# Opening three feed-forward layers with two of the seven products of many blocks

## The chip, the cores and the metric

The kernel runs on one core of a Trainium2 chip. The metric is the device time of one execution in microseconds (us). Engine names are those of the profile: PE is TensorE (matrix products), DVE is VectorE, ACT is ScalarE, POOL is GpSimd, SP is SyncE, which here only issues DMAs.

## What is computed

Two layers of a network on 256 context and 512 latent tokens of width 1024. Each layer is feed-forward, mixer, feed-forward, each behind a modulation by shift, scale and gate vectors made from a conditioning vector, and each closed by a layer norm. The part that matters here:

```python
def swiglu(h, w_in, w_out):
    a, b = jnp.split(h @ w_in, 2, axis=-1)
    return (jax.nn.silu(a) * b) @ w_out

def ffn_substep(x, mods, w_in, w_out, g, b):
    shift, scale, gate = mods
    y = swiglu(modulate(x, shift, scale), w_in, w_out)
    return layer_norm(ALPHA * x + MACARON * gate * y, g, b)
...
m_lat = jnp.split((c_act @ w_ada[layer] + b_ada[layer])[:, None, :], N_MOD, axis=-1)
```

The hidden width is 2816, so `w_in` has 2 x 22 blocks of 128 columns. There are four feed-forward layers, called here (0,0), (0,1), (1,0) and (1,1). The first three work on all 768 tokens, the last on the 512 latent ones.

## The kernel before

All products are made in three passes: each fp32 operand is split into a rounded part (ACT cast, L117) and the remainder (DVE subtraction, L119), and `mm3` issues h*h, h*l and l*h (L157 to L159). `xh` and `xl` hold the split input, 8 tiles of 128 rows by 768 tokens.

The first half of a feed-forward layer makes gate and up rows of 22 hidden blocks. A **plain** block is 2 x 8 x 3 products on all tokens, made in the two token halves of the layer norm before (512 and 256 tokens; 256 and 256 in (1,1)). The other blocks are made by one level of Strassen's scheme in Winograd's form (`seven`): seven products of 4 x 3 matmuls on half the tokens (384; 256 in (1,1)) instead of eight. Its weight sums are made per block on POOL (`ahead`, L673 to L675, and L684), two blocks ahead, then split by ACT and DVE (`operands`); its input sums once per layer (`sums_of_inputs`: POOL adds at L650, DVE subtractions at L648, splits). Results leave PSUM by ACT copies and DVE additions (L712, L711), and `put` multiplies gate and up (L583, L587), which keeps one token half in `spare` tiles and stores the other (`late_g`).

Before the change, (0,1) and (1,0) open with 4 plain blocks and (1,1) with 5. The reason is the layer norm of the step before: its second token half is still being normalized (`pending`, drained by `settle`) while PE works on the first half, and the input sums need both.

Beside the products, `ada` makes the modulation vectors: per block of 128 columns a 512 KB load and one DVE product with a sum (L185) for each of one or two conditioning vectors. A list of sections for each layer says which vectors are made beside its first half (tiles `spare`) and which beside its second half (tiles `six`). Beside the first half two blocks of such columns are made per hidden block, until the list is done.

Every engine executes its own instructions in a fixed order, which is set when the program is built; the orders shown below are of built programs.

Of the kernel before, what the change touches and what calls it, by code (L numbers as in the profile page):

```python
# [12 lines left out]
F32 = mybir.dt.float32  # L13
F32R = mybir.dt.float32r
BF16 = mybir.dt.bfloat16
AF = mybir.ActivationFunctionType
# [3 lines left out]
P = 128  # L20
D = 1024
KB = D // P
NCTX = 256
NLAT = 512
NT = NCTX + NLAT
# [17 lines left out]
class Net:  # L43
    def __init__(self, tc, ctx, ins, out):
# [35 lines left out]
        self.RB = None  # L80
# [143 lines left out]
    def start(self, pool):  # L224
# [33 lines left out]

        w = lambda q: [load(self.ins["w_ada0"][q, i]) for i in range(KB // 2)]
# [6 lines left out]
        for j in range(KB):  # L266
# [8 lines left out]
            self.split(self.xh[:, j, :], self.xl[:, j, :], x_)  # L275
            if j % 2 and q < 4:
                columns(q, quarter)
# [21 lines left out]
    def layer_norm(self, half, halves, aff, nxt, ax_new, r_of, s1, done, table):  # L299
        nc = self.nc  # L300
# [26 lines left out]
        for j in range(KB):  # L327
            r = r_of(half, j)
            nc.vector.tensor_mul(out=r, in0=r, in1=rs[:, :n])  # L329
            if nxt is not None:  # L330
# [8 lines left out]
                self.split(self.xh[:, j, c0:c1], self.xl[:, j, c0:c1], h[:, :n])  # L339
            g, b = aff[:, 0, j:j + 1], aff[:, 1, j:j + 1]  # L340
# [27 lines left out]
    def out_phase(self, pool, nk, wsrc, gload, halves, gate, l, i, nxt, r_of, table=None, keep=False, ada=iter(())):  # L368
# [3 lines left out]
        aff = self.affine(l, i, nxt)  # L372
        ax_new = None
        if nxt is not None:
            self.n += 1
            ax_new = self.dram.tile([P, KB, NT], F32, name=f"ax{self.n}")
        nh = nk // 2
# [33 lines left out]
        for n_step, (half, kk) in enumerate(steps):  # L411
# [33 lines left out]
            if half:  # L445
                for _ in norm:
                    pass
            s1 = self.sums(n)
# [34 lines left out]
    def residual(self, r, j, c0, c1):  # L483
# [5 lines left out]
        nc.scalar.mul(out=r, in_=r, mul=ALPHA)  # L489

# [66 lines left out]
    def ffn(self, l, p, halves, nxt, ada=((), ()), table=None, first_of_all=False):  # L557
# [5 lines left out]
        plain = 4 if n > 512 else 5  # L563
        in_ada, out_ada = (list(a) for a in ada)
        with ExitStack() as st:
# [72 lines left out]
            def sums_of_inputs():  # L638

                t1 = [self.spare(pool)[:, :2 * m].rearrange("p (k c) -> p k c", k=2) for _ in range(2)]  # L640
# [3 lines left out]
                for k in range(4):  # L644
                    hi = lambda K, N: B(K, N)[0][:, k, :].bitcast(F32)
                    lo = lambda K, N: B(K, N)[1][:, k, :].bitcast(F32)
# [6 lines left out]
                    a = t1[k // 2][:, k % 2, :]  # L653
                    sub(a, b12, hi(0, 0))
                    sub(a, a, lo(0, 0))
# [22 lines left out]
            def operands(raw, sums):  # L678
# [4 lines left out]
                w = self.pair(raw[0], 1024)  # L683
                nc.gpsimd.tensor_sub(out=a12, in0=a12, in1=sums[:, 512:])  # L684
                yield part(w, 0), part(w, 1)
# [8 lines left out]

            def seven(x, now, coming, before):
# [4 lines left out]

                def grow(ps, w, b):

                    first = ps is None
                    ps = self.ps()[:, :m] if first else ps
                    for k in range(4):
                        ks = slice(k * P, (k + 1) * P)
# [677 lines left out]
```

## Time and profile before

| what | before |
|---|---|
| median of 3 runs (lowest to highest) | 2761.87 us (2758.68 to 2762.24) |
| the profiled execution | 2759.16 us |
| its span, first to last instruction | 2757.4 us |
| mean granted TensorE clock in it | 0.992 |
| PE busy | 2662.5 us, 97% |
| DVE busy | 1964.8 us, 71% |
| ACT, POOL busy | 1219.8 us, 891.0 us |

Busy shares are means over stages with different limits. Here the stage that matters is the first half of a feed-forward layer, and in it the time of one block on each engine.

### The profile page before, as it was taken

To read this page: it belongs to the slowest core of one execution; us is meant where nothing else is said; L and a number is where in the kernel's file an instruction comes from. 1 tells how busy PE (TensorE), PEld (TensorE's weight loads), DVE (VectorE), ACT (ScalarE), POOL (GpSimd) and SP (SyncE) were. 2 spreads that over 40 slices of the span, in tenths; PEclk is the share of its full clock that TensorE was granted. 3 is DMA by queue.
4 is the path that set the end of the run, shared out by engine and by line. 5 is a ranking of instruction groups with operands and counts; after the bars stand their busy time and mean duration, and the time that the engine had idled before them with its cause. 6 is when DMAs were issued, how large, how long until landed. Compare 5 with 4: busy or idle time off the path is not lost. (4 is left out here: it accounts for less than half of the span.)

```text
span 2757.4 us, 43916 instructions
## 1 busy us (share of the span) xinstructions
PE 2662.5 (97%) x17372; PEld 2429.0 (88%) x17372; DVE 1964.8 (71%) x2917; ACT 1219.8 (44%) x1919; POOL 891.0 (32%) x686
## 2 busy tenths in 40 slices
PE   8999999999989999999999999999999998999997
PEld 6999988987778789999889999988887777999997
DVE  4899677847764779977786676556727776787665
ACT  3433433634442544343254444423534655555554
POOL 2545300522210564440044444201422211466302
PEclk9999999999999999999999999999999999999998
DMA  6343266521104334426653432265521012423563
GB/s 250 138 154 123 94 233 233 202 87 68 46 22 166 109 132 147 140 88 221 218 199 121 166 127 79 92 231 194 204 77 47 35 39 85 134 102 119 173 218 116
DMA packets 138770, 374.20 MB, mean 136 GB/s; under 512 B 16066, under 2 KB 47170, under 8 KB 138564
## 3 DMA queue, kind: packets, MB, share of 16 engines
q1 hardware_dynamic: 136832, 370.21, 38.3%
q8 instruction: 136, 2.23, 0.3%
q10 hardware_dynamic: 1732, 1.20, 0.2%
q14 instruction: 70, 0.57, 0.1%
HBM read 337.78 MB, written 33.56 MB: 135 GB/s over the span
## 5 line engine op out<-in xcount | busy, mean ns | idle before, releaser
L117 ACT CAST r4h<-raw 128x1024 fp32r<-128x1024 f32 (+1 forms) x322 | 332.7, 1035 | 627.5 <-PE ps L158 320.3
L157 PE MATMUL ps<-xh,r4h 128*128 128x512 f32 (+2 forms) x1732 | 584.3, 339 | 11.1 <-ACT xh L117 7.7
L158 PE MATMUL ps<-xl,r4h 128*128 128x512 f32 (+2 forms) x1732 | 580.8, 336 | 0.5 <-DVE xl L119 0.4
L159 PE MATMUL ps<-xh,r4l 128*128 128x512 f32 (+2 forms) x1732 | 580.5, 336 | 0.4 <-DVE r4l L119 0.4
L119 DVE TENSOR_TENSOR r4l<-raw,r4h 128x1024 fp32r<-128x1024 f32 (+1 forms) x306 | 374.2, 1225 | 223.0 <-ACT r4h L117 161.7
L157 PEld LDWEIGHTS ps<-xh,r4h 128*128 128x128 f32 x1732 | 327.1, 189 | 40.6 <-ACT xh L117 10.2
L158 PEld LDWEIGHTS ps<-xl,r4h 128*128 128x128 f32 x1732 | 327.9, 189 | 23.0 <-DVE xl L119 2.0
L159 PEld LDWEIGHTS ps<-xh,r4l 128*128 128x128 f32 x1732 | 327.6, 189 | 22.1 <-DVE r4l L119 0.8
L157 PE MATMUL ps<-six,r4h 128*128 128x384 f32 (+1 forms) x852 | 278.5, 327 | 6.6 <-ACT c L712 6.5
L157 PE MATMUL ps<-r4h 128*128 128x512 f32 (+1 forms) x768 | 275.7, 359 | 1.1 <-DVE g L827 1.1
L158 PE MATMUL ps<-six,r4h 128*128 128x384 f32 (+1 forms) x852 | 276.1, 324 | 0.0
L159 PE MATMUL ps<-r4h,r4l 128*128 128x512 f32 (+1 forms) x768 | 275.5, 359 | 0.2
L159 PE MATMUL ps<-six,r4l 128*128 128x384 f32 (+1 forms) x852 | 275.5, 323 | 0.0
L158 PE MATMUL ps<-r4l,r4h 128*128 128x512 f32 (+1 forms) x768 | 275.2, 359 | 0.0
L159 PE MATMUL ps<-r4h,spare 128*128 128x256 f32 (+1 forms) x896 | 262.2, 293 | 10.1 <-DVE spare L119 10.0
L157 PE MATMUL ps<-r4h,spare 128*128 128x256 f32 (+1 forms) x896 | 265.5, 296 | 4.0 <-ACT spare L117 4.0
L158 PE MATMUL ps<-r4l,spare 128*128 128x256 f32 (+1 forms) x896 | 261.3, 292 | 0.0
L684 POOL TENSOR_TENSOR raw<-raw,late 128x512 f32<-128x512 f32 x71 | 93.6, 1318 | 400.7 <-DVE r4l L119 397.2
L119 DVE TENSOR_TENSOR r4l<-late,r4h 128x1024 fp32r<-128x1024 f32 x71 | 106.1, 1494 | 115.1 <-PE ps L158 95.5
L159 PEld LDWEIGHTS ps<-r4h,spare 128*128 128x128 f32 x896 | 174.4, 195 | 13.6 <-DVE spare L119 11.7
L157 PEld LDWEIGHTS ps<-r4h,spare 128*128 128x128 f32 x896 | 174.5, 195 | 8.6 <-ACT spare L117 4.6
L185 DVE SCALAR_TENSOR_TENSOR trash<-spare 128x1024 bf16<-128x1024 f32 x112 | 179.3, 1603 | 1.3 <-DMA spare<-in_w_ada 1.3
(289 smaller groups left out, 5637.9 us busy)
## 6 DMA issues: line engine op xcount, KB each, us to landing
raw<-in_w_ffn_in SPq DMA_DIRECT2D x176, 512.0 KB, 3.6
raw<-in_w_ffn_out SPq DMA_DIRECT2D x176, 512.0 KB, 4.1
spare<-in_w_ada SPq DMA_DIRECT2D x80, 512.0 KB, 5.6
six<-in_w_ada SPq DMA_DIRECT2D x64, 512.0 KB, 5.5
g<-late_g SPq DMA_DIRECT2D x88, 128.0 KB, 2.1
six<-g SPq DMA_DIRECT2D x44, 256.0 KB, 3.8
raw<-in_w_in_even SPq DMA_DIRECT2D x20, 512.0 KB, 3.5
raw<-in_w_in_odd SPq DMA_DIRECT2D x16, 512.0 KB, 3.4
```

What stands on the lines that cost most here:

```text
L117: self.copied = self.nc.scalar.copy(out=h, in_=src)
L119: eng.tensor_sub(out=l, in0=src, in1=h.bitcast(F32))
L157: mm(out=ps, lhsT=h, rhs=xh, start=first, stop=False)
L158: mm(out=ps, lhsT=h, rhs=xl, start=False, stop=False)
L159: mm(out=ps, lhsT=l, rhs=xh, start=False, stop=last)
L185: nc.vector.scalar_tensor_tensor(out=self.tmp("trash").bitcast(BF16), in0=r, scalar=1.0, in1=self.c_bc[v], op0=ALU.mult, op1=ALU.mult, acc ...
L684: nc.gpsimd.tensor_sub(out=a12, in0=a12, in1=sums[:, 512:])
```

## The change

In (0,1), (1,0) and (1,1) there are no plain blocks any more. The layer opens with the first two of the seven products, A11*B11 and A12*B21, of 10 blocks (14 in (1,1)); both need only the first half of the tokens. The first product is copied and stored to DRAM (`p1s`), the sum of both goes through the activation into the gate's place (`G`). Then `five` makes the other five products of these blocks, with the first one loaded back, and `seven` the rest. The layer norm (and the start of the kernel) also stores the unsplit input to DRAM (`whole`), from which `sums_of_inputs` loads four quarters in place of POOL's additions and one of the DVE subtractions. The sections of modulation vectors are dealt out anew, and the layer norm's `affine` is made at the end of the first token half, since its inputs can now be made beside the same layer's second half.

```diff
-        plain = 4 if n > 512 else 5
+        plain, opened = (4, 0) if first_of_all else (0, 10 if n > 512 else 14)
...
-                    for t, q in ((b12, (0, 1)), (b22, (1, 1)), (b21, (1, 0))):
-                        nc.gpsimd.tensor_add(out=t, in0=hi(*q), in1=lo(*q))
+                    for t, (K, N) in ((a, (0, 0)), (b12, (0, 1)), (b22, (1, 1)), (b21, (1, 0))):
+                        nc.sync.dma_start(out=t, in_=self.whole[:, K * 4 + k, cols[N]])
...
-                    sub(a, b12, hi(0, 0))
-                    sub(a, a, lo(0, 0))
+                    sub(a, b12, a)
...
-                w = self.pair(raw[0], 1024)
+                if not opened:
+                    w = self.pair(raw[0], 1024)
                 nc.gpsimd.tensor_sub(out=a12, in0=a12, in1=sums[:, 512:])
...
+            def opening(sums):
+                wt = [self.weights(ws[2 * x]) for x in range(3)]
...
+                def first_product(x):
+                    X[x] = grow(None, part(x, 0), B(0, 0))
+                    t = self.tmp("p1")[:, :m]
+                    copy(t, X[x])
+                    nc.sync.dma_start(out=p1s[:, x, :], in_=t)
+
+                first_product(0)
+                for x in range(opened):
+                    if x + 1 < opened:
+                        first_product(x + 1)
+                    grow(X[x], part(x, 1), B(1, 0))
+                    if x < 2:
+                        self.settle(None if x else 9)
+                    else:
...
+                                    nc.scalar.activation(out=G(i)[:, 0, :m], in_=X.pop(i), func=AF.Silu)
+                        self.settled = None
+                        next(sums, None)
+                    if x + 3 < opened:
+                        wt.append(self.weights(ws[2 * x + 6]))
...
+            def five(x, now, coming, before):
+
+                (S2, S1), S4 = now[0][:2]
+                if x % 2 == 0:
+                    load_p1(x + 2)
+                p1 = p1_of.pop(x)
+                u2, p5 = (self.tmp("c")[:, :m] for _ in range(2))
+                X = grow(None, S2, made[2])
+                add(u2, p1, X)
+                before()
...
+                Y = grow(None, S1, made[1])
+                add(p5, p1, Y)
+                more(coming)
+                grow(X, S3, made[3])
+                add(p5, p5, X)
+                next(ada, None)
+                more(coming)
+                grow(Y, S4, B(1, 1))
+                add(u2, u2, Y)
+                nc.scalar.activation(out=u2, in_=u2, func=AF.Silu)
+                put(x, m, n, u2, p5)
+
+                def rest():
+                    grow(X, A22, made[4])
+                    add(p1, p1, X)
+                    put(x, 0, m, G(x)[:, 0, :m], p1)
...
-        net.ffn(0, 1, FULL, (1, 0, (LAT, CTX)), (each(0, 8, 9) + each(1, 0, 2), each(1, 2, 5)), SILU)
-        net.ffn(1, 0, FULL, (1, 3, (LAT, CTX)), (each(1, 5, 7), each(1, 7, 9)))
+        net.ffn(0, 1, FULL, (1, 0, (LAT, CTX)), (each(0, 8, 9) + each(1, 0, 1), each(1, 1, 3)), SILU)
+        net.ffn(1, 0, FULL, (1, 3, (LAT, CTX)), (each(1, 3, 5), each(1, 5, 8)))
...
-        net.ffn(1, 1, LATS, None)
+        net.ffn(1, 1, LATS, None, (each(1, 8, 9), ()))
```

How this moves instructions shows in the order on three places. The first is DVE in layer (0,1), in a hidden block that makes modulation vectors beside it. Before, twelve of the fourteen rows of one `seven` block (a split of `raw` and a product `L583 spare<-c,ps` stand ahead of them): L119 splits weights, L711 adds out of PSUM, L185 makes modulation vectors, L583 and L587 multiply gate and up.

```order
L119 TENSOR_TENSOR r4l<-raw,r4h 128x1024
L711 TENSOR_TENSOR c<-c,ps 128x384
L119 TENSOR_TENSOR r4l<-late,r4h 128x1024
L185 SCALAR_TENSOR_TENSOR trash,mod_0_104<-spare 128x1024
L711 TENSOR_TENSOR c<-c,ps 128x384
L185 SCALAR_TENSOR_TENSOR trash,mod_1_105<-spare 128x1024
L119 TENSOR_TENSOR r4s<-raw,r4s 128x512
L711 TENSOR_TENSOR c<-c,ps 128x384
L185 SCALAR_TENSOR_TENSOR trash,mod_0_104<-spare 128x1024
L583 TENSOR_TENSOR spare<-c 128x128
L587 TENSOR_TENSOR late_g<-c 128x256
L185 SCALAR_TENSOR_TENSOR trash,mod_1_105<-spare 128x1024
```

After it, twelve of the fifteen rows of one `five` block (two L715 additions out of PSUM and the split `r4l<-late,r4h` stand ahead of them); L715 is the addition, L594 and L598 the products of gate and up.

```order
L594 TENSOR_TENSOR spare<-spare 128x384
L715 TENSOR_TENSOR c<-spare,ps 128x384
L119 TENSOR_TENSOR r4s<-raw,r4s 128x512
L715 TENSOR_TENSOR c<-c,ps 128x384
L185 SCALAR_TENSOR_TENSOR trash,mod_0_104<-spare 128x1024
L185 SCALAR_TENSOR_TENSOR trash,mod_1_105<-spare 128x1024
L119 TENSOR_TENSOR r4l<-raw,r4h 128x1024
L715 TENSOR_TENSOR c<-c,ps 128x384
L185 SCALAR_TENSOR_TENSOR trash,mod_0_104<-spare 128x1024
L594 TENSOR_TENSOR spare<-c 128x128
L598 TENSOR_TENSOR late_g<-c 128x256
L185 SCALAR_TENSOR_TENSOR trash,mod_1_105<-spare 128x1024
```

One split of 1024 columns has left the block, two additions out of PSUM have come, and all four L185 stand in the shorter block as in the longer one: two blocks of modulation columns, two vectors each, in blocks 0 to 7 of (0,1) and of (1,0).

The second place is DVE in (1,1), in a block without modulation vectors: before, one `seven` block.

```order
L119 TENSOR_TENSOR r4l<-raw,r4h 128x1024
L583 TENSOR_TENSOR spare<-c,ps 128x256
L119 TENSOR_TENSOR r4l<-raw,r4h 128x1024
L711 TENSOR_TENSOR c<-c,ps 128x256
L119 TENSOR_TENSOR r4l<-late,r4h 128x1024
L119 TENSOR_TENSOR r4s<-raw,r4s 128x512
L711 TENSOR_TENSOR c<-c,ps 128x256 x2
L587 TENSOR_TENSOR late_g<-c 128x256
```

After it, one `five` block of (1,1).

```order
L715 TENSOR_TENSOR c<-spare,ps 128x256
L598 TENSOR_TENSOR late_g<-c 128x256
L119 TENSOR_TENSOR r4l<-late,r4h 128x1024
L715 TENSOR_TENSOR spare<-spare,ps 128x256
L119 TENSOR_TENSOR r4s<-raw,r4s 128x512
L594 TENSOR_TENSOR spare<-spare 128x256
L715 TENSOR_TENSOR c<-spare,ps 128x256
L119 TENSOR_TENSOR r4l<-raw,r4h 128x1024
L715 TENSOR_TENSOR c<-c,ps 128x256 x2
```

Again one split has gone and two additions have come, in a block of five products in place of seven; the product that took an operand from PSUM (L583) now takes both from SBUF (L594). POOL has its four instructions per block in both.

The third place is the DMA queue on SP near the end of the opening of (0,1): L661 loads quarters of `whole` for the input sums, L733 stores first products, L124 loads the weights of an opening block. Nothing of it stood there before.

```order
L352 DMA ax_8187<-late 128x256
L733 DMA p1s_8873<-p_9098 128x384
L661 DMA spare<-whole_8188 128x384
L661 DMA b<-whole_8188 128x384 x3
L661 DMA spare<-whole_8188 128x384
L733 DMA p1s_8873<-p_9162 128x384
L661 DMA b<-whole_8188 128x384 x3
L661 DMA spare<-whole_8188 128x384
L661 DMA b<-whole_8188 128x384
L733 DMA p1s_8873<-p_9222 128x384
L661 DMA b<-whole_8188 128x384 x2
L124 DMA raw<-in_w_ffn_in 128x1024
```

The weights of one of the last two opening blocks are issued behind most of the loads for the input sums, which themselves stand behind the last stores of the layer norm.

## Rows read from the trace of the kernel before

**Rows 1.** The page, part 1: engine, busy us (share of the span) xinstructions.
```profile
PE 2662.5 (97%) x17372; PEld 2429.0 (88%) x17372; DVE 1964.8 (71%) x2917; ACT 1219.8 (44%) x1919; POOL 891.0 (32%) x686
```

**Rows 2.** Windows: stretch, length, busy (x instructions) by engine, PEclk, DMA share, GB/s.
```profile
1465.50:1485.50 20.00, 20.00 (x88) 16.25 (x87) 12.03 (x29) 11.11 (x26) 7.58 (x9) 1.00 0.13 46
...
1200.00:1260.00 60.00, 60.00 (x343) 60.00 (x342) 34.34 (x42) 24.47 (x37) 19.53 (x13) 1.00 0.23 79
2460.00:2560.00 100.00, 100.00 (x837) 100.00 (x837) 78.26 (x90) 54.02 (x90) 60.90 (x40) 1.00 0.34 119
1021.60:1167.80 146.20, 145.94 (x824) 144.50 (x823) 133.36 (x181) 57.06 (x87) 72.79 (x40) 1.00 0.42 146
...
1001.00:1011.00 10.00, 7.10 (x41) 6.78 (x40) 4.82 (x6) 6.76 (x12) 7.91 (x6) 1.00 0.50 171
```

**Rows 3.** DVE by line and shape, ten `seven` blocks (1021.6 to 1167.8): busy, mean ns | idle.
```profile
L185 DVE SCALAR_TENSOR_TENSOR trash<-spare 128x1024 bf16<-128x1024 f32 x39 | 61.3, 1571 | 0.0
L119 DVE TENSOR_TENSOR r4l<-raw,r4h 128x1024 fp32r<-128x1024 f32 x20 | 24.3, 1217 | 0.0
L119 DVE TENSOR_TENSOR r4s<-raw,r4s 128x512 fp32r<-128x512 f32 x10 | 17.7, 1769 | 0.0
L711 DVE TENSOR_TENSOR c<-c,ps 128x384 f32<-128x384 f32 x29 | 15.8, 546 | 0.7 <-PE ps L159 0.6
L119 DVE TENSOR_TENSOR r4l<-late,r4h 128x1024 fp32r<-128x1024 f32 x10 | 12.4, 1243 | 12.2 <-PE ps L158 8.2 <-ACT c L712 1.8 <-PE ps L159 1.5
```

**Rows 4.** DVE by line and shape, whole span: the same operations elsewhere.
```profile
L185 DVE SCALAR_TENSOR_TENSOR trash<-six,late 128x1024 bf16<-128x1024 f32 x112 | 131.8, 1224 | 29.5 <-DMA six<-in_w_ada 29.3
...
L119 DVE TENSOR_TENSOR r4l<-spare,r4h 128x512 fp32r<-128x512 f32 x11 | 7.5, 686 | 0.0
```

**Rows 5.** POOL by line and shape, 1200 to 1260 us.
```profile
L684 POOL TENSOR_TENSOR raw<-raw,late 128x512 f32<-128x512 f32 x4 | 5.2, 1297 | 30.9 <-DVE r4l L119 30.9
L673 POOL TENSOR_TENSOR late<-raw 128x512 f32<-128x512 f32 x3 | 3.9, 1294 | 0.1
```

**Rows 6.** Timeline of DVE, one `seven` block of (1,1): start, length, instruction [idle before].
```profile
2484.16 1.23 DVE L119 TENSOR_TENSOR r4l<-late,r4h 128x1024 fp32r<-128x1024 f32 x1 [1.33 <-PE ps L158]
2485.30 1.78 DVE L119 TENSOR_TENSOR r4s<-raw,r4s 128x512 fp32r<-128x512 f32 x1
2487.01 0.74 DVE L711 TENSOR_TENSOR c<-c,ps 128x256 f32<-128x256 f32 x2
2488.53 1.25 DVE L587 TENSOR_TENSOR late_g<-c 128x256 f32<-128x256 f32 x1 [0.79 <-ACT c L736]
...
2494.22 1.23 DVE L119 TENSOR_TENSOR r4l<-late,r4h 128x1024 fp32r<-128x1024 f32 x1 [1.33 <-PE ps L158]
```

**Rows 7.** Timeline of POOL, the same block.
```profile
2484.60 1.93 POOL L673 TENSOR_TENSOR late<-raw 128x512 f32<-128x512 f32 x1 [0.67 <-DMA raw<-in_w_ffn_in]
2486.61 1.63 POOL L674 TENSOR_TENSOR late<-late,raw 128x512 f32<-128x512 f32 x1
2488.20 1.29 POOL L675 TENSOR_TENSOR raw<-raw 128x512 f32<-128x512 f32 x1
```

**Rows 8.** Timelines: last norm splits (DVE), first plain product of (1,0) (PE).
```profile
935.88 0.72 DVE L119 TENSOR_TENSOR xl<-h,xh 128x512 fp32r<-128x512 f32 x1 [0.61 <-ACT xh L117]
...
957.11 0.76 DVE L119 TENSOR_TENSOR xl<-h,xh 128x256 fp32r<-128x256 f32 x2 [0.82 <-ACT xh L117]
...
1463.54 0.39 PE L157 MATMUL ps<-xh,r4h 128*128 128x512 f32 x1
...
1486.12 0.76 DVE L119 TENSOR_TENSOR xl<-h,xh 128x256 fp32r<-128x256 f32 x2 [0.82 <-ACT xh L117]
```

**Rows 9.** DMA issues: out<-in, queue, count, size, median us from issue to landing.
```profile
ax<-late SPq DMA_DIRECT2D x40, 128.0 KB, 1.7
late<-ax SPq DMA_DIRECT2D x40, 128.0 KB, 3.1
```

More of the change, by code (lines that the diff above doesn't have):

```diff
@@ L257, in load @@
             return t
+        self.whole = self.whole_input()
         w = lambda q: [load(self.ins["w_ada0"][q, i]) for i in range(KB // 2)]
@@ L275, in start @@
             self.split(self.xh[:, j, :], self.xl[:, j, :], x_)
+            nc.sync.dma_start(out=self.whole[:, j, :], in_=x_)
             if j % 2 and q < 4:
@@ L339, in layer_norm @@
                 self.split(self.xh[:, j, c0:c1], self.xl[:, j, c0:c1], h[:, :n])
+                if whole is not None:
+                    nc.sync.dma_start(out=whole[:, j, c0:c1], in_=h[:, :n])
             g, b = aff[:, 0, j:j + 1], aff[:, 1, j:j + 1]
@@ L376, in out_phase @@
             ax_new = self.dram.tile([P, KB, NT], F32, name=f"ax{self.n}")
+        self.whole = self.whole_input() if nxt is not None and nxt[1] in (0, 6) else None
         nh = nk // 2
@@ L447, in out_phase @@
                     pass
+            if not half:
+                aff = self.affine(l, i, nxt)
             s1 = self.sums(n)
@@ L693, in operands, with grow @@
                 yield part(w, 0), part(w, 1)
-            def seven(x, now, coming, before):
[L701 to L706, printed above, removed]
-                        self.mm3(ps, w[0][:, ks], w[1][:, ks], b[0][:, k, :], b[1][:, k, :], first and k == 0, k == 3,
-                                 True)
-                    return ps
-                add = lambda o, a, b: nc.vector.tensor_add(out=o, in0=a, in1=b)
-                copy = lambda o, a: nc.scalar.copy(out=o, in_=a)
-                more = lambda of: of[0].extend(itertools.islice(of[1], 1))
+            def grow(ps, w, b):
+                first = ps is None
+                ps = self.ps()[:, :m] if first else ps
+                for k in range(4):
+                    ks = slice(k * P, (k + 1) * P)
+                    self.mm3(ps, w[0][:, ks], w[1][:, ks], b[0][:, k, :], b[1][:, k, :], first and k == 0, k == 3, True)
+                return ps
@@ L750, in room @@
                 return sums[0][:, x % 2 * 1024:x % 2 * 1024 + 1024]
-            self.project(ws[:2 * plain], halves, ps_of, done, 4 if n > 512 else 6,
-                         self.start(pool) if first_of_all else None, pool, sums_of_inputs())
+            if opened:
+                opening(sums_of_inputs())
+                load_p1(0)
+            else:
+                self.project(ws[:2 * plain], halves, ps_of, done, 4, self.start(pool), pool, sums_of_inputs())
             t1, made[1] = made[1], B(0, 1)
@@ L758, in ffn @@
             ada = self.ada(in_ada, [room_of(), room_of()], room_of, 2 * (HB - 6 - plain)) if in_ada else iter(())
-            block = lambda x: ([], operands(*ahead(x, room(x))) if x < HB else iter(()))
-            now, coming, before = ([], operands(*made["next"])), block(plain + 1), lambda: None
-            now[0].extend(itertools.islice(now[1], 3))
+            block = lambda x: ([], operands(*ahead(x, room(x)), x < opened) if x < HB else iter(()))
+            now, coming, before = ([], operands(*made["next"], bool(opened))), block(plain + 1), lambda: None
+            now[0].extend(itertools.islice(now[1], 2 if opened else 3))
             for x in range(plain, HB):
-                then, before = seven(x, now, coming, before)
+                then, before = (five if x < opened else seven)(x, now, coming, before)
                 now, coming = coming, then
```

39 lines of the change are left out of this document (31 added, 8 removed).

## The prediction, made before the changed kernel ran

> **What bounds the kernel now.** I read the page first: PE is busy for 97% of the span [rows 1], so a change pays only by taking matmuls away or by ending PE's waits, and it costs wherever another engine becomes slower than PE. Then the windows, for the pace of PE inside a block [rows 2]: 88 matmuls of 512 columns in 20.0 us are 0.227 us each, 343 of 384 columns in 60.0 us 0.175, 837 of 256 columns in 100.0 us 0.1195. These stretches hold no wait of PE. The fourth window covers ten `seven` blocks of (0,1) that make modulation vectors: PE 145.94 of 146.2 us, but DVE 133.36. So DVE needs 13.3 us of a block of 14.6. The reader should see that PE is the bound there by 1.3 us only.
>
> Next I asked what fills DVE. In these ten blocks L185 takes 1571 ns and the split of `r4s` 1769 [rows 3]; where POOL does little the same operations take 1224 and 686 [rows 4]. The timelines of one block of (1,1) show why [rows 6, 7]: `r4s` starts at 2485.30 and ends at 2487.08, POOL's L673 ends at 2486.53 and its L674 ends 1.2 us after `r4s`. The 256-column product at 2488.53 takes 1.25 us beside L675. The two L711 at 2487.01, which read PSUM, take their normal 0.37 each beside L674. So a DVE instruction with both operands in SBUF and a two-operand POOL instruction run one after the other, while DVE's additions out of PSUM run beside POOL. The Trainium skill says the same of the hardware ("SBUF — State Buffer", section "SBUF: two separate sides"): DVE and GpSimd share a port pair that an instruction with two SBUF inputs holds as "an exclusive lock, not a bandwidth split". The trace agrees with it in these rows. By that rule alone, this change is bad where it packs the same POOL and DVE work into less PE time: the floors of 13.5 and 8.6 us below would hold whatever the order, and the sum at these floors would be +65 us.
>
> **PE's work.** (0,1) and (1,0): a plain block is 48 x (0.227 + 0.1195) = 16.65 us, a block of seven products 84 x 0.175 = 14.7; four blocks save 7.8 us a layer. (1,1): I take three plain blocks in halves of 256 (96 x 0.1195 = 11.5) and two in 512 (48 x 0.227 = 10.9) against 84 x 0.1195 = 10.0; saved 6.0. Together **-21.6 us**. An opening block is 24 matmuls, 4.2 us (2.9 in (1,1)), a `five` block 60, 10.5 us (7.2).
>
> **The five blocks that make modulation vectors, (0,1) and (1,0).** DVE per block, from start to start (recorded lengths overlap by 0.08): splits 1.15 + 1.14 + 0.61 [rows 3, 4, 6], four L185 with their reads of the sum, 4 x 1.22 = 4.9 [rows 4], five additions of 384 at 0.47 = 2.35 [rows 3], three products, about 0.47 + 0.20 + 0.33 by their columns. Sum 11.15 us, already above PE's 10.5. POOL keeps its four instructions, 4 x 1.25 = 5.0 us when alone [rows 5]. Of these 13.5 us cannot overlap (8.5 of DVE out of SBUF plus 5.0), and POOL can hide only beside the additions and the reads of sums, 2.65 us. Bounds: all of it used, 11.15 + 5.0 - 2.65 = 13.5; none, 16.1. In the `seven` blocks DVE waited 4 x (1.571 - 1.217) + (1.769 - 0.686) = 2.5 us for POOL [rows 3, 4] (1.217 is what a split of the same width takes), so 2.5 of 5.0 was hidden, in 2.2 us of additions and reads plus 1.2 of idle time, 74%. With the same share 2.0 is hidden and a block takes **14.2 us**, 3.7 over PE's. The excess cannot be saved up: PE's fourth product writes the bank that DVE's addition `p5` must have read, one product earlier, where `seven` left that to an ACT copy. Two blocks of columns per hidden block, 16 blocks in two layers: 16 x 3.7 = **+59 us** (16 x 3.0 = 48 to 16 x 5.6 = 90). Blocks 8 and 9 and all `seven` blocks keep PE's pace: 6.3 us of DVE and 5.0 of POOL fit in 10.5 with the additions beside POOL.
>
> **The five blocks of (1,1).** DVE: 1.15 + 1.14 + 0.61, five additions and two products of 256 at 0.34 [rows 6]: 5.3 us. POOL 5.0. Not to be overlapped: 3.6 + 5.0 = 8.6 against PE's 7.2. In the `seven` block DVE waited 1.9 us (late_g 0.8, r4s 1.1), so 88% of its additions and idle time (1.4 + 2.1) hid POOL; the same share of 1.7 us leaves 5.3 + 5.0 - 1.5 = **8.8 us** (8.6 to 10.3). Ten blocks: +16. Four blocks carry two L185 with one vector each, +2.4 on DVE: 11.2, +16. Together **+32 us** (29 to 57).
>
> **The entry into the five blocks.** The first of them needs the input sums, and these need the end of the layer norm, a store and a load. (1,0): norm's last split ends at 1486.9 [rows 8]; store and load 1.7 + 3.1 [rows 9]; 28 subtractions of 0.47 = 13.2; two weight splits 2.3; half of six POOL instructions in between, 3.75; the first split 1.15: 1512. PE starts at 1463.5 [rows 8] and has 42 us of opening and 1.6 of statistics: 1507. It waits 5 us. (0,1): 957.9 [rows 8] + 25.2 = 983; PE cannot finish second products before the first half's last split at 936.6 [rows 8], when three first products (6.3 us) may be done: 972. It waits 11, where it lost 2.9 at the entry of `seven` before (7.10 busy of 10.0 [rows 2]). (1,1) by the same chain: 2. Together **+15 us** (0 to 45; the top if the last opening weights, which are queued on SP behind the loads of `whole`, cost each layer 10 more).
>
> **At nothing.** The first products' stores and loads and the second load of A11 and A12 lie under a DMA share of 0.23 to 0.42 [rows 2]; ten ACT copies lie under an ACT that is busy 5.7 of 14.6 us. `affine`, some ten instructions of 8 columns, 1 us of DVE at the turn of the halves; uncovered it would be 1 us in each of six layer norms. POOL's 36 and 12 input additions go, out of a stage that the entry above already prices without them. The stores of `whole` hold the norm's `h` 1.7 us longer, of seven buffers. The first layer: 0 +- 3. Where PE falls behind, each layer's PE may be one product (2.1 us) ahead of the additions when the last slow block ends: **-6**.
>
> **Sum.** -21.6 + 59 + 32 + 15 - 6 = +78 us on the profiled 2759.2, which lies 0.1% under the median of the runs: **2837 us**, 2.8% slower.
>
> **Rivals.** *PE stays the bound (faster).* DVE and POOL would have to finish a `five` block with modulation vectors in PE's 10.5 us; then only -21.6 is left: 2738. For it speaks that PE never waits in `seven`, at 13.3 us of DVE; against it that DVE's own instructions alone make 11.15. It decides at a block time of about 11: -21.6 + 15 + 16 x 0.4. *POOL costs DVE nothing more (same).* DVE's own time bounds: 16 x 0.65 + 4 x 0.5 = +12, entry 15, less 6: 2759. Against it are the waits in [rows 3, 6]. *The openings run dry (slower still).* Weights behind the loads of `whole` on SP: 10 us more in three layers, 2867. The order speaks for it, the prefetch of three blocks against.
>
> **How the numbers follow.** Chances: the forecast 0.65, its own range 2790 to 2870; dry openings 0.17; POOL costs nothing 0.07; PE bound 0.11. The range 2772 to 2885 leaves out the two low cases, 0.18, and little above. No change means within 0.2% (5.5 us), about what a measurement of this kernel can tell. Faster: 0.11 and a quarter of the 0.07, 0.13. Same: 0.04. Slower: 0.83.
>
> **What would show it.** In `five` blocks of (0,1) and (1,0) with L185, DVE busy all the time, a period of 14 us and not 10.5, PE waiting for L715 and L119; behind them, `seven` at 14.7. In (1,1) a period near 8.8, POOL and DVE together always busy. A gap of PE where the opening ends. Wrong it is if L185 and the splits come down to 1.22 and 0.69 us beside POOL, if the period is 10.5, or if PE's waits lie in the openings. A PE that idles a quarter of the time may also be granted a lower clock, which this sum leaves out.

## The result and the profile after

The changed kernel takes 2905.3 us (2902.9 to 2913.4) against 2760.3 (2757.5 to 2762.2) beside it on the same chip: 1.053 times, interval 1.0515 to 1.0541. It is slower, as forecast, but by 145 us in place of 78, and it lies above the range. Its profiled execution took 2913.4 us, the longest of its four.

All of the difference lies in the first halves of the three layers. By the first product of a layer and the first of its second half, in the two traces:

| layer | before | after | difference |
|---|---|---|---|
| (0,1) | 349.4 us | 396.8 us | +47.4 |
| (1,0) | 336.0 us | 379.6 us | +43.6 |
| (1,1) | 233.5 us | 297.9 us | +64.4 |

A single trace scatters by some us: in two runs below whose edits touch (1,1) alone, the first half of (0,1) took 392.6 and 390.1 us.

The page of the changed kernel, part 1 (columns as in [rows 1]):

```profile
PE 2691.8 (92%) x17312; PEld 2464.2 (85%) x17312; DVE 2074.4 (71%) x3042; ACT 1228.3 (42%) x1918; POOL 916.5 (31%) x690
```

Here and below, the time of a block runs from the product `late_g` of the block before to its own. Windows of the changed kernel (columns as in [rows 2]): seven `five` blocks of (0,1) with modulation vectors, fourteen blocks of (1,1) (the last of them a `seven`), about nine of these without vectors, and the three openings up to the first of the five products.

```profile
1013.80:1113.50 99.70, 80.77 (x427) 76.91 (x426) 98.82 (x139) 20.86 (x27) 44.34 (x26) 0.97 0.51 164
2540.90:2692.30 151.40, 117.54 (x860) 113.37 (x859) 126.47 (x159) 44.81 (x62) 89.43 (x56) 0.92 0.42 137
2595.00:2690.00 95.00, 74.18 (x524) 72.38 (x523) 73.96 (x87) 28.34 (x39) 54.26 (x34) 0.87 0.32 102
920.80:995.40 74.60, 56.67 (x249) 52.42 (x249) 56.18 (x93) 44.47 (x88) 42.25 (x41) 0.84 0.61 206
1510.00:1571.10 61.10, 51.01 (x250) 48.81 (x249) 48.00 (x78) 36.86 (x73) 26.84 (x24) 0.89 0.62 204
2464.60:2528.10 63.50, 47.36 (x334) 44.94 (x333) 45.96 (x79) 39.17 (x84) 23.13 (x24) 0.89 0.64 208
```

In the first row DVE is busy for 98.8 of 99.7 us and PE for 80.8: seven blocks, 14.24 us each, where the fourth window of [rows 2] has ten `seven` blocks at 14.6 with PE busy throughout. In (1,1), rows two and three, nobody is busy all the time. The granted clock, 1.00 in all of [rows 2], falls to 0.84 in an opening; a mean of 0.84 between the two levels is a third of the time at 1.2 GHz.

DVE by line and shape in the seven blocks of the first row, the answer to [rows 3]:

```profile
L185 DVE SCALAR_TENSOR_TENSOR trash<-spare 128x1024 bf16<-128x1024 f32 x30 | 47.2, 1593 | 0.0
L594 DVE TENSOR_TENSOR spare<-spare 128x384 f32<-128x384 f32 x7 | 10.4, 1485 | 0.0
L119 DVE TENSOR_TENSOR r4s<-raw,r4s 128x512 fp32r<-128x512 f32 x7 | 8.5, 1207 | 0.0
L715 DVE TENSOR_TENSOR c<-c,ps 128x384 f32<-128x384 f32 x14 | 7.6, 542 | 0.9 <-PE ps L159 0.9
L715 DVE TENSOR_TENSOR c<-spare,ps 128x384 f32<-128x384 f32 x14 | 7.6, 541 | 0.0
```

L185, `r4s` and L594 have both operands in SBUF and are long beside POOL; the additions out of PSUM are not.

Timeline of DVE for one block of (1,1) without vectors, the answer to [rows 6]:

```profile
2607.12 1.54 DVE L598 TENSOR_TENSOR late_g<-c 128x256 f32<-128x256 f32 x1
2608.59 2.31 DVE L119 TENSOR_TENSOR r4l<-late,r4h 128x1024 fp32r<-128x1024 f32 x1
2610.82 0.41 DVE L715 TENSOR_TENSOR spare<-spare,ps 128x256 f32<-128x256 f32 x1
2611.16 1.42 DVE L119 TENSOR_TENSOR r4s<-raw,r4s 128x512 fp32r<-128x512 f32 x1
2612.50 1.48 DVE L594 TENSOR_TENSOR spare<-spare 128x256 f32<-128x256 f32 x1
2613.91 0.41 DVE L715 TENSOR_TENSOR c<-spare,ps 128x256 f32<-128x256 f32 x1
2614.24 1.21 DVE L119 TENSOR_TENSOR r4l<-raw,r4h 128x1024 fp32r<-128x1024 f32 x1
2615.37 0.41 DVE L715 TENSOR_TENSOR c<-c,ps 128x256 f32<-128x256 f32 x1
2617.34 0.42 DVE L715 TENSOR_TENSOR c<-c,ps 128x256 f32<-128x256 f32 x1 [1.56 <-PE ps L159]
2619.68 0.42 DVE L715 TENSOR_TENSOR c<-spare,ps 128x256 f32<-128x256 f32 x1 [1.93 <-PE ps L159]
```

This is a ring: each engine waits for the other in turn. The addition at 2613.91 reads the bank (the part of PSUM that holds one product) that PE's fourth product will write; ahead of it stand `r4s` and L594, 2.9 us, long because of POOL. Later DVE itself waits for PE, 1.56 and 1.93 us. PE's waits from 2595 to 2690 are these (us in total, times, longest):

```profile
PE ps L157 <- DVE c L715: 20.8, 8, 4.8
```

The opening of (1,0). DVE's groups between 1536 and 1572 us that make the input sums and split them:

```profile
L119 DVE TENSOR_TENSOR six<-b,six 128x384 fp32r<-128x384 f32 x12 | 8.0, 676 | 0.0
L659 DVE TENSOR_TENSOR b<-b 128x384 f32<-128x384 f32 x8 | 6.1, 757 | 0.2 <-DVE spare L659 0.2
L659 DVE TENSOR_TENSOR b<-b,spare 128x384 f32<-128x384 f32 x4 | 3.9, 967 | 0.1
L659 DVE TENSOR_TENSOR spare<-b,spare 128x384 f32<-128x384 f32 x4 | 3.3, 823 | 0.0
```

PE's waits in the same opening:

```profile
PE ps L157 <- ACT p L716: 7.2, 2, 5.0
PE ps L157 <- ACT r4h L117: 2.6, 1, 2.6
```

The first line of the same answer in (0,1) and in (1,1):

```profile
PE ps L157 <- ACT p L716: 10.8, 5, 4.3
PE ps L157 <- ACT p L716: 12.9, 4, 6.7
```

PE is held by ACT's copies of first products (L716) and by weights (`r4h`). The longest wait in (1,0), 5.0 us, ends in this window, where ACT is busy all the time with the norm's `h` and `xh`, which stand ahead of the copy in its order:

```profile
1531.00:1537.00 6.00, 0.98 (x5) 0.66 (x4) 3.63 (x10) 6.00 (x16) 6.00 (x8) 0.83 0.65 219
```

Where the opening ends, the forecast had PE wait for the input sums. It does not: in none of the three layers does PE wait at the first of the five products; its last wait lies 6, 12 and 5 us ahead of it. The sums end 5 us ahead in (0,1) and (1,0) and 14 us ahead in (1,1). Their 28 instructions take DVE 21.3 us as recorded, about 19 without the overlap of recorded lengths (0.08 each); the forecast had 13.2 for them and 3.75 for POOL in between. Alone one takes 0.55 us, as an addition out of PSUM does; beside POOL's sums of weights it takes up to 1.6.

### The profile page after: what moved, and what is told of

Same layout as the page of the kernel before. It is cut to its first block, busy times and chain, and to the rows that moved or that the text cites. A ratio compares the mean times of both kernels' runs of the same rounds, so it can differ in the third digit from the quotient of the medians.

```text
span 2911.4 us, 44461 instructions
## 1 busy us (share of the span) xinstructions
PE 2691.8 (92%) x17312; PEld 2464.2 (85%) x17312; DVE 2074.4 (71%) x3042; ACT 1228.3 (42%) x1918; POOL 916.5 (31%) x690
## 4 chain that ended last, share of the span: by engine, by line
PE 67%; DVE 17%; issue 6%; ACT 5%; POOL 2%; DMA 2%; SPq 0%; POOLq 0%; DVEq 0%; ACTq 0%
PE ps L157 20%; PE ps L158 20%; PE ps L159 19%; DVE trash L185 4%; DVE r4l L119 2%; DVE spare L594 1%; DVE c L715 1%; PE ps L1337 1%; PE ps L1338 1%; PE ps L1339 1%; PE ps L1308 1%; PE pss L1236 1%; ACT e L1240 1%; DVE late L1014 1%; DMA spare<-in_w_ada 1%
## 5 line engine op out<-in xcount | busy, mean ns | idle before, releaser
L157 PE MATMUL ps<-xh,r4h 128*128 128x384 f32 (+2 forms) x1616 | 552.9, 345 | 50.2 <-ACT p L716 30.9
L119 DVE TENSOR_TENSOR r4l<-raw,r4h 128x1024 fp32r<-128x1024 f32 (+1 forms) x314 | 390.9, 1247 | 257.8 <-ACT r4h L117 175.2
L158 PE MATMUL ps<-xl,r4h 128*128 128x384 f32 (+2 forms) x1616 | 546.5, 339 | 0.0
L159 PE MATMUL ps<-xh,r4l 128*128 128x384 f32 (+2 forms) x1616 | 544.9, 339 | 1.0 <-DVE r4l L119 1.0
L157 PE MATMUL ps<-six,r4h 128*128 128x384 f32 (+1 forms) x1008 | 334.2, 332 | 49.4 <-DVE c L715 47.7
L157 PEld LDWEIGHTS ps<-xh,r4h 128*128 128x128 f32 x1616 | 310.9, 193 | 80.3 <-ACT p L716 34.8
L159 PE MATMUL ps<-six,r4l 128*128 128x384 f32 (+1 forms) x1008 | 329.9, 329 | 8.0 <-DVE r4l L119 8.0
L158 PE MATMUL ps<-six,r4h 128*128 128x384 f32 (+1 forms) x1008 | 331.0, 328 | 0.0
L159 PEld LDWEIGHTS ps<-xh,r4l 128*128 128x128 f32 x1616 | 311.3, 193 | 18.4 <-DVE r4l L119 1.8
L157 PEld LDWEIGHTS ps<-six,r4h 128*128 128x128 f32 x1008 | 194.7, 193 | 58.2 <-DVE c L715 49.4
L694 POOL TENSOR_TENSOR raw<-raw,late 128x512 f32<-128x512 f32 x84 | 131.0, 1560 | 326.1 <-DVE r4l L119 312.8
L682 POOL TENSOR_TENSOR late<-raw 128x512 f32<-128x512 f32 x84 | 127.0, 1511 | 332.2 <-DMA raw<-in_w_ffn_in 290.9
L119 DVE TENSOR_TENSOR r4l<-late,r4h 128x1024 fp32r<-128x1024 f32 x84 | 135.6, 1615 | 103.0 <-PE ps L158 87.1
L159 PEld LDWEIGHTS ps<-six,r4l 128*128 128x128 f32 x1008 | 195.9, 194 | 10.3 <-DVE r4l L119 10.3
```

What stands on the lines that cost most here:

```text
L119: eng.tensor_sub(out=l, in0=src, in1=h.bitcast(F32))
L157: mm(out=ps, lhsT=h, rhs=xh, start=first, stop=False)
L158: mm(out=ps, lhsT=h, rhs=xl, start=False, stop=False)
L159: mm(out=ps, lhsT=l, rhs=xh, start=False, stop=last)
L682: nc.gpsimd.tensor_add(out=s1, in0=a21, in1=a22)
```

## The experiments

Every edit is made on the changed kernel. All totals are medians; "before" was run beside each and lay between 2759.7 and 2762.4 us.

**POOL's sums left out.** For blocks made by five products `ahead` returns the loaded weights in place of the sums, and the L694 subtraction is left out.

```diff
+                if x < opened:
+                    return raw, raw[0]
                 a11, a21, a22 = raw[0][:, :512], raw[1][:, :512], raw[1][:, 512:]
```

> Leaves out POOL's weight sums of the blocks made by five products (four POOL instructions a block): the splits take the loaded weights in their place, so DVE, ACT, PE and the loads keep their instructions. Theory 1 (DVE and POOL exclude each other, and their sum sets the block): five blocks with four L185 go from 14.2 to DVE's own 11.2 to 11.5, blocks of (1,1) without L185 from 10.9 to PE's 7.2 to 7.6, with L185 from 11.3 to 7.8. That is 45 + 35 + 14 = about 95 us less, 2810 us. Theory 2 (the round trip PE, DVE, PE sets the block, POOL only delays single instructions in it): the blocks with L185 stay above 13, those of (1,1) come down by the 2 us that r4s and L594 lose beside POOL, to about 9: 50 us less or fewer, 2855 us.

The kernel took 2800.7 us, 105 less. Most blocks with vectors came to 10.78 us, those of (1,1) to 7.25 in the steady stretch, PE's pace. DVE in eight blocks of (0,1):

```profile
L185 DVE SCALAR_TENSOR_TENSOR trash<-spare 128x1024 bf16<-128x1024 f32 x31 | 37.9, 1250 | 0.0
L594 DVE TENSOR_TENSOR spare<-spare 128x384 f32<-128x384 f32 x8 | 5.7, 713 | 0.0
L119 DVE TENSOR_TENSOR r4s<-raw,r4s 128x512 fp32r<-128x512 f32 x8 | 5.7, 712 | 0.0
```

The same instructions took 1250, 713 and 712 ns in place of 1593, 1485 and 1207. POOL's four instructions cost a block 3.5 us of its 14.2. With them 44 of the 64 us went that the first half of (1,1) had lost (253.8 us here).

**The same sums on DVE.**

```diff
-                nc.gpsimd.tensor_add(out=s1, in0=a21, in1=a22)
+                eng = nc.vector if x < opened else nc.gpsimd
+                eng.tensor_add(out=s1, in0=a21, in1=a22)
```

and so for the other three.

> From the changed kernel; the four weight sums of every block made by five products are computed by DVE in place of POOL, nothing else changes. Theory 1 (a DVE instruction with two operands in SBUF and POOL's wait for each other, and POOL's 1.25 us for 512 columns is what the block pays): DVE alone needed 10.8 us a block with four L185, and the same sum costs it about 0.61 us: 10.8 + 2.4 = 13.2 us in place of 14.2; in (1,1) 5.3 + 2.4 = 7.7 to 8.5 in place of 10.9 and 11.3. About 16 x 1.0 + 14 x 3 = 58 us less, 2847 us. Rival (the two engines do work side by side to a large part, and POOL only delays some instructions): DVE takes the sums on top, 14.2 + 2.4 = 16.6 us in (0,1) and (1,0), 38 us more there, and (1,1) stays near 10.5: 2940 us.

The kernel took 2875.6 us, 30 less. Blocks 1 to 7 with vectors took 13.8 us: more work on the engine that was full made them shorter, since a sum takes DVE 0.69 us where POOL takes 1.29 [rows 5]. But block 8 then took 16.2 us in both layers, in place of 13.4 and 13.5, so over blocks 1 to 9 less than 2 us a layer were left, no more than such stretches scatter between traces. Why block 8 grew was not followed up. The gain came elsewhere: 8.0 and 4.6 us up to the first `late_g` of (0,1) and (1,0), and 22 in the first half of (1,1), where DVE had not been full and blocks came to 9.5 on average. There only part came, since DVE, in order, now waits for the loads of the weights whose sums it makes; in the combination below this is 9.5 us in 80:

```profile
L683 DVE TENSOR_TENSOR late<-raw 128x512 f32<-128x512 f32 x8 | 5.5, 692 | 9.5 <-DMA raw<-in_w_ffn_in 9.5
```

**Modulation vectors elsewhere.**

```diff
-(each(0, 8, 9) + each(1, 0, 1), each(1, 1, 3)), SILU)
+((), each(0, 8, 9) + each(1, 0, 2)), SILU)
-(each(1, 3, 5), each(1, 5, 8)))
+(each(1, 5, 8), each(1, 2, 5)))
-net.ffn(1, 1, LATS, None, (each(1, 8, 9), ()))
+net.ffn(1, 1, LATS, None, ((), each(1, 8, 9)))
```

> From the changed kernel (2905.3 us), the modulation vectors are taken out of the five blocks of (0,1) and (1,1) and made beside the second half of the layer; in (1,0) each block keeps two products L185 in place of four (one vector, three sections). Theory 1, a block's time is DVE's and POOL's work that cannot overlap: five blocks of (0,1) go from 14.2 to about 10.7 us, those of (1,0) to 11.7, the first four of (1,1) from 11.8 to 10.9. About 33 + 22 + 4 = 59 us less, 2846 us. Theory 2, the wait of the fourth product for the addition L715 comes from the place of that addition in DVE's order and L185 only fills time that would be lost anyway: periods stay above 13 us, 2890 us or more. If the second half of (0,1), which gets 48 products L185 in place of 32, becomes longer than 120 us, some of the gain is given back there.

The kernel took 2865.6 us, 40 less. Blocks of (0,1) came to 11.6 us, those of (1,0) to 12.8, and the second halves stayed at 119.5 us. So theory 1 holds in direction, but without any L185 a block is still above PE's 10.5. DVE is busy for only 8.9 us of it, the 6.3 of the working and 2.6 more beside POOL, which is what theory 1 allows; for the rest it waits, 1.7 us for PE and 1.2 for ACT, and PE waits for the addition in its turn. So what keeps the block over 10.5 here are waits of the ring, not a sum of work.

**The addition first.** L594 is held back, and both it and the split `r4s` are issued after the addition.

```diff
-                add(p5, p1, Y)
-                more(coming)
+                first = add(p5, p1, Y)
+                with self.tc.issue_after(first.ins):
+                    held()
+                    more(coming)
```

> Same work; in DVE's order the addition L715 that reads the bank wanted by the fourth product stands ahead of L594 of the block before and of the split r4s, not behind them. Theory 2 (round trip): in (1,1) the wait of PE for that addition loses about 2.9 us less the part that moves elsewhere, blocks 4 to 13 go from 10.9 to about 8.8 us: 20 us less there; in (0,1) and (1,0), where DVE has no idle time, no change, 14.2 us. About 2885 us. Theory 1 (sum of DVE and POOL): no change anywhere, 2905 us within 5.

The kernel took 2886.6 us, 19 less. Blocks with vectors stayed at 14.23 us; the ten `five` blocks of (1,1) that hold no L185 fell from 10.7 to 9.6 on average. Both parts are as the round trip has it; DVE and POOL's sum alone would have moved neither. (The granted clock in the last nine blocks rose with it, from 0.87 to 0.98; what the order alone is worth is not separated.) The three blocks behind those with vectors, which theory 2 did not mention, took 34.5 and 34.8 us in (0,1) and (1,0), against 37.6 to 41.3 in traces with the order as it was.

**A useless product, and its control.** In (1,1) PE makes one product again ahead of the fourth.

```diff
+                if n <= 512:
+                    grow(None, S3, made[3])
                 grow(Y, S4, B(1, 1))
```

> From the changed kernel; in the five blocks of (1,1) PE makes one product (12 matmuls of 256 columns, 1.4 us) once more into a bank that nothing reads, just ahead of the fourth product, where PE waits. It asks what the lower granted clock (0.69 to 0.84 in these blocks) costs. If PE's matmuls at the lower clock lengthen the round trip: the clock stays near 1.0 and the blocks do not get longer in spite of 20 us more work, perhaps 5 to 10 us shorter in all. If the clock costs nothing because PE waits anyway: periods unchanged or longer by up to 1.4 us a block, 0 to 20 us more.

The kernel took 2898.1 us. The window of nine blocks of (1,1) without vectors, the last of them a `seven`:

```profile
2589.80:2675.90 86.10, 81.37 (x662) 79.54 (x661) 70.58 (x90) 29.73 (x41) 55.32 (x35) 1.00 0.39 122
```

The blocks take 9.6 us on average, six of them 9.32 or 9.33, at a clock of 1.00 and with 1.4 us of work more in each `five` block. One thing in DVE's order had moved with it: `late_g` stood ahead of the next block's first addition. This was then done alone:

```diff
-                add(u2, p1, X)
+                with self.tc.issue_after(made["late_g"].ins) if n <= 512 and x else nullcontext():
+                    add(u2, p1, X)
```

> The control to filler, without its useless product: from the changed kernel, in the five blocks of (1,1) the product late_g of a block stands ahead of the next block's first addition L715 in DVE's order, as it came to stand in filler; nothing else. If filler's 9.32 us a block come from PE being kept at the full clock, blocks 5 to 13 stay at 10 to 11 us here and the granted clock stays near 0.87. If they come from this place in DVE's order, blocks come to about 9.3 us here too, and the lower clock cost nothing there.

The kernel took 2909.8 us. The same nine blocks, with the same order on DVE as in the run before:

```profile
2589.00:2685.00 96.00, 75.83 (x544) 74.18 (x544) 75.52 (x91) 29.80 (x42) 57.14 (x36) 0.89 0.31 102
```

They take 10.7 us each, at a clock of 0.89. So what shortened the blocks, by 1.1 us each, was PE kept at work. By the two windows PE's useful work took 0.7 us a block less at the higher clock (75.8 us against 81.4 less some 12 of useless work), and DVE's instructions beside POOL 0.5 less (75.5 against 70.6). Whether the second follows from the first is not shown.

**The openings.** Five edits, and the time from a layer's first product to the first `late_g` (the last column is the whole kernel). The second row has the openings unchanged: in (0,1) this time scatters by 4 us between traces, in the other two by 1 or less.

| kernel | (0,1) | (1,0) | (1,1) | total |
|---|---|---|---|---|
| as changed | 91.9 | 76.2 | 76.3 | 2905.3 |
| `late_g` first, in (1,1) alone (above) | 88.1 | 76.3 | 77.1 | 2909.8 |
| norm one product later | 88.2 | 78.4 | 77.3 | 2902.8 |
| and first products two ahead | 86.3 | 79.8 | 77.0 | 2904.0 |
| weights five ahead | 86.7 | 73.5 | 78.9 | 2903.1 |
| sums from the network's input | 91.3 | 76.4 | 76.0 | 2908.3 |
| half a product more in PE's waits | 91.1 | 79.0 | 80.8 | 2906.8 |
| POOL's sums left out (above) | 83.8 | 71.4 | 70.9 | 2800.7 |
| POOL's sums on DVE (above) | 83.9 | 71.7 | 73.9 | 2875.6 |

```diff
-                    if x < 2:
-                        self.settle(None if x else 9)
+                    if x < 3:
+                        self.settle((9, 1, None)[x])
```

> Same work; in the openings the rest of the layer norm is put into the program one product later, so that the copy of the fourth first product stands ahead of the norm's last activations on ACT. Theory 3: the openings are late because PE waits for that copy (gaps of 5.4 us at 1531.0 and 7.0 us at 2481.1): the first of the five products comes 5 us earlier in (0,1) and (1,0) and 7 in (1,1), 2888 us. Rival: the input sums end only 3.5 us ahead of the first of the five products in (0,1) and (1,0), so they set the start: 3 us a layer at most there, and 7 or less in (1,1), 2895 to 2905 us.

In no layer did the first `late_g` come earlier than in the second row, and in (1,0) it came 2 us later: theory 3 failed.

With this edit and:

```diff
+                first_product(1)
                 for x in range(opened):
-                    if x + 1 < opened:
-                        first_product(x + 1)
+                    if x + 2 < opened:
+                        first_product(x + 2)
```

> From the changed kernel, same work; in the openings first products run two blocks ahead of second ones in place of one, and the norm's rest is put into the program one product later (as in norm_later), so every copy L716 has a whole product more until PE needs its bank. Theory 3 (PE's waits for the copies, 10.8, 7.2 and 12.9 us, make the openings late): most of these waits go, the first block's product late_g comes 5 to 10 us earlier in each layer, 2885 us. Theory 3c (norm, store, load and input sums set the end): the same time, 2900 us.

The copies did come earlier, but PE then waited for casts of weights (6.9 us in (0,1), 6.3 in (1,0)).

```diff
-                wt = [self.weights(ws[2 * x]) for x in range(3)]
+                wt = [self.weights(ws[2 * x], spare=pool if x > 2 else None) for x in range(5)]
```

> From the changed kernel; in the openings weights are loaded and split five blocks ahead in place of three (two of them in spare buffers), so the loads of the last five blocks no longer stand behind the loads of the input sums on SP's queue and their splits not behind the sums on DVE. Theory 3b (the openings are late because the last weights are): the first of the five products comes 5 us earlier in each layer, 2890 us. Rival 3c (the chain of norm, store, load and 28 subtractions sets it, 35 us from the norm's end to the first of the five products): at most 2 us a layer, 2900 to 2905 us.

The first of the five products came 10 and 12 us earlier in (0,1) and (1,0), but the input sums then ended 6.4 us later in (0,1), and the first `late_g` gained 1 to 5 us there, by which trace one compares with, 3 in (1,0) and nothing in (1,1).

```diff
-                        nc.sync.dma_start(out=t, in_=self.whole[:, K * 4 + k, cols[N]])
+                        nc.sync.dma_start(out=t, in_=ins["x"][:, K * 4 + k, cols[N]])
```

> From the changed kernel; the input sums load the network's input in place of the layer's stored input, so they wait neither for the norm nor for a store (wrong values in the sums; all instructions and loads are there). Theory 3c: the start of the five products, which now waits for nothing of the norm, is set by PE's 42 us (41 in (1,1)) and comes 12 us or more earlier in each layer, 2865 us. Theory 3d (PE itself is late: it waits for the norm's first half, for copies and for weights, at a lower granted clock): less than 4 us a layer, 2895 us.

Nothing moved. DVE's and ACT's orders are the same instructions in the same places here, so the sums still stand behind the norm on DVE. That excludes the store and load as the cause, not the place of the sums.

```diff
+                    dead = self.ps()[:, :m]
+                    for k in range(2):
...
+                        self.mm3(dead, w[0][:, ks], w[1][:, ks], b[0][:, k, :], b[1][:, k, :], k == 0, k == 1, True)
                     grow(X[x], part(x, 1), B(1, 0))
```

> From the changed kernel; in the openings PE makes half a product (6 matmuls, 1.05 us, 0.72 us in (1,1)) into a bank that nothing reads just ahead of each second product: 10.5 us of work more in each opening. The openings of the changed kernel are 73.5, 61.1 and 63.5 us long; PE's own work at the full clock is 43.6, 43.6 and 41.8, its waits make 17.9, 10.0 and 16.2, and half of its time at the lower clock 12.0, 6.9 and 6.9. Theory 4 (the lower clock is a cost of its own, and it comes from the waits): the work lies in the waits and the time at the lower clock falls, the openings get 0 to 5 us shorter in spite of it, 2895 us. Rival (the lower clock is a mere companion of the waits, which are set by other engines): the openings stay as long within 2 us where all of the filler lies in waits, and are up to 10 us longer where not, 2905 to 2930 us.

Up to the first of the five products it took 75.3, 64.6 and 67.4 us, 2 to 4 more than as changed, for 10 us more of work each, at a clock of 0.89, 0.97 and 0.92 in place of 0.84, 0.89 and 0.89. So the useless work lay mostly in waits, and the higher clock brought no shorter opening: theory 4 fell. What the lower clock costs an opening by itself is not shown, as the added work takes PE's time too.

**Put together.** The vectors elsewhere, the sums on DVE, the addition first, the norm later and the weights five ahead, with 10, 10 and 14 blocks opened, and with 14 in (0,1) too:

> Everything together on the changed kernel: modulation vectors moved as in ada_moved, weight sums of five blocks on DVE, the addition first, the norm later, weights five ahead; 10, 10 and 14 blocks opened. By theory 1 the five blocks come to PE's pace in (0,1) (DVE 6.3 + 2.4 = 8.7 against 10.5), to 11.1 in (1,0), to about 7.8 in (1,1): from ada_moved's 2865.6 us 10 + 14 + 33 less, and 5 to 15 less in the openings: about 2795 us. What is left over the kernel before is then in the openings alone.

> As comb10w, but 14 blocks opened in (0,1) too. If PE has idle time in the opening because the norm and the input sums are not ready (theory 3c), four more opening blocks fill it: the opening of (0,1) grows from 73 us by less than the 16.8 us that they need, and four blocks behind it take 10.5 us in place of 14.8: up to 12 us less than comb10w, 2783 us. If the opening is late because PE itself is (its own products, its clock), the opening grows by 16.8 us and nothing is gained: as comb10w.

These two took 2803.6 and 2809.6 us. `five` blocks came to 10.8, 11.7 and 8.7 us on average in the three layers. From the first product of (0,1) to its first `late_g` it took 77.6 us with 10 opened and 93.7 with 14: 4.0 us for each block more, where PE's own work is 4.2. So more opening work does not fill idle time there.

(1,1) had the largest loss left, 30 us, so the next two kernels leave it plain.

```diff
+        plain, opened = (4, 0) if first_of_all else (0, 10) if n > 512 else (5, 0)
```

> A version that could match the kernel before: 10 blocks opened in (0,1) and (1,0), five plain blocks in (1,1) as before; no modulation vectors beside any five blocks (64, 56 and 56 products L185 beside the second halves of the first three layers), weight sums of five blocks on DVE, the addition first, weights five ahead, first products two ahead. From comb10w's times by layer: (0,1) 351 and (1,0) 346 us less 0.3 and 0.7 us for each of ten five blocks gives 348 and 339, (1,1) 233 as before, 2 to 4 us more in the second half of (1,0): 2762 to 2770 us, about as before. If the remaining waits are set by DVE in the five blocks also without L185: 2775 us.

> As two_opened, but first products run one block ahead as in comb10w, and the splits of the fourth quarter (xl from spare, ahead of the first five block) are on DVE in place of POOL, for which PE waited 8.5 and 4.0 us. (0,1): 351 us of comb10w less 2 for the wait and 3 for ten five blocks, 346 to 349; (1,0): 346 less 2 and 6, 338 to 341; (1,1) 231 as in two_opened: 2758 to 2765 us, the same as before. If DVE, which takes four more splits at the entry, is late there instead: 2770 us.

They took 2776.5 us (1.0048 times before, interval 1.0029 to 1.0066) and 2767.2 us (1.0024, 1.0014 to 1.0035). Even so, two openings cost more than the 15.6 us that they save.

Last, the change without any opening:

```diff
+        plain, opened = 4 if n > 512 else 5, 0
```

> The rest of the change without its openings: no block opened, 4, 4 and 5 plain blocks and the sections of modulation vectors as before, but the unsplit input stored and its quarters loaded for the input sums in place of POOL's additions, and affine at the end of the first half. (1,1) took 231 us in this form in both two_opened kernels against 233.5 before; (0,1) lost 2.9 us at the entry of its seven products before. If the loads in place of POOL's additions are a gain of their own: 2 to 6 us less than before, 2754 to 2758 us. If the stores and loads cost as much as they save: 2760 us within 3.

It took 2754.4 us, 0.9972 times before (0.9961 to 0.9982): 0.3% faster than the kernel before, and 13 us faster than the better of the two with openings. The stored input, its loads in place of POOL's additions and the later `affine` are a small gain; PE's wait of 2.9 us at the entry of `seven` in (0,1), the gap in the last of [rows 2], is gone. The window in its place:

```profile
990.00:1003.00 13.00, 13.00 (x76) 11.89 (x76) 5.16 (x9) 5.73 (x10) 4.16 (x4) 1.00 0.57 204
```

The openings, with the dealing of vectors that goes with them, therefore cost 151 us.

## Why the prediction was right in direction and wrong in size

- **Blocks with modulation vectors: right.** 14.24 us against 14.2, DVE never idle. That POOL's work holds up DVE's work out of SBUF was shown by leaving POOL's sums out (10.78).
- **"Blocks 8 and 9 ... keep PE's pace": failed.** They took 13.35, 13.35, 13.47 and 11.57 us, 10 us more in all (6 in the two traces with the same blocks). The working added up DVE and POOL, 6.3 + 5.0 with the additions beside POOL, and as a sum that holds: with no L185 at all DVE was busy for 8.9 us. The block still took 11.6, since DVE and PE wait for each other in turn, and that wait has no term.
- **The five blocks of (1,1): mechanism half right, size wrong.** The three behind the first, in which the L185 stand, took 11.5 us on average against 11.2. The ten others took 10.7 against 8.8, 19 us more. I priced a throughput, DVE and POOL added up; the runs showed a round trip PE, DVE, PE, which shortens with the addition first (9.6) and with PE kept at work (9.6 against 10.7). (The top of this term's range, 57, comes to 53 by its own figures.)
- **The entry: failed; this is the largest part of the miss.** It took 73.5, 61.1 and 63.5 us from a layer's first product to the first of the five, against 61.5, 48.5 and 44 in the working: 44 us more, where the rival of dry openings had 30. The step that failed is "PE ... has 42 us of opening and 1.6 of statistics", with no wait inside it, and the ten ACT copies put at nothing. PE waited 17.9, 10.0 and 16.2 us inside the openings, of this 10.8, 7.2 and 12.9 for the copies and only 4.2, 2.6 and 1.4 for weights, which were the rival's mechanism; the rest is PE's own work at the lower clock. "PE's waits lie in the openings" was one of the prediction's own signs of being wrong. The wait that the prediction did price, 11, 5 and 2 us for the input sums where the opening ends, was not there. The price of the sums themselves was 2 us short (19 against 13.2 + 3.75).
- **Why the openings are late stays open in part.** Where copies or weights were moved ahead, PE waited elsewhere: in (0,1) and (1,0) copies, weights and sums, all on queues that run in order, end within some 5 us of each other. Two single edits brought the first `late_g` forward in all three layers beyond the scatter: POOL's sums left out (by 8, 5 and 5 us) and made on DVE (8, 5 and 2). Most of that lies behind the first of the five products, in the first `five` block (18.4, 15.1 and 12.8 us to its `late_g`; 12.6, 12.6 and 9.8 without POOL's sums).
- **The lower clock, left out of the sum.** 153 us at the lower level in the changed kernel against 47 before, by the clock's records in the two traces. In (1,1) keeping it up paid; in the openings no gain was found.
- **The credit of 6 us** showed only in part: the first `seven` blocks took 14.59, 13.81 and 9.61 us in place of 14.80, 14.80 and 10.06, 1.7 in all. Together 44 + 19 + 10 + 4 = 77 us, against the 76 between the forecast and the profiled execution. That the blocks with vectors came out within 0.1 us is partly luck: DVE alone took 0.4 less than forecast (10.78 against 11.15) and POOL cost 0.4 more (3.5 against 3.0).

## What to carry to other kernels

When products are taken away from PE, price the shorter block on every engine that runs in order, and then follow the ring: which instruction frees the bank that PE wants, and what stands ahead of it. Two engines that exclude each other are one resource: there, giving the slower one's work to the faster can pay, here 30 us. Take a price from a row with the same neighbour at work: a sum of 384 columns took 0.55 us alone and up to 1.6 beside POOL. And price the waits of a stretch whose engines each run in order, even where each engine's busy share is low: the copies that were put at nothing held PE for 31 us.

## What the runs showed of the hardware

Useless matmuls made a stage faster: 1.4 us more of PE work in each `five` block of (1,1) shortened it from 10.7 to 9.6 us, with the granted clock at 1.00 in place of 0.89. And an elementwise sum of 512 columns took 1.29 us on POOL [rows 5] and 0.69 on DVE. The Trainium skill ("GPSIMD Engine Reference", section "Engine selection") gives a factor of about 2 for it; this case's rows agree, at 1.9.
